# A hybrid diffusion-transformer step on one core: transposes by DMA on 16-bit halves, 33 groups of seven products, and new tables

## The chip, the cores and the metric

The kernel runs on one core of a Trainium2 chip. The metric is the device time of one execution in microseconds (us); before the change it is 1346.45 us, the median of three runs (1346.03 to 1346.79).

## The reference

One layer over two groups of 128 tokens of width 2048 (a prompt and a noisy sample), in float32:

```
(shift1, scale1, gate1, shift2, scale2, gate2) = SiLU(cond) @ w_ada + b_ada      # adaLN, per group
h  = RMSNorm(x) * (1 + scale1) + shift1
q_A, k_A, v_A, q_B, k_B, v_B, gate_A, gate_B = split(h @ w_in)                    # 8704 columns
o_A, o_B = two attentions (window / neighbourhood), with context keys
merged = (sigmoid(gate_A) * (o_A @ w_br_a) + sigmoid(gate_B) * (o_B @ w_br_b)) @ w_out
x  = x + gate1 * merged
h2 = RMSNorm(x) * (1 + scale2) + shift2
x  = x + gate2 * (relu(h2 @ w_up) ** 2 @ w_down)                                  # 2048 -> 8192 -> 2048
```

The outputs are both groups' x and the new keys and values.

## The kernel before, in words

**Steps.** All weights are streamed once, in 456 steps of one tile of 128 x 1024 numbers (512 KB: two rows of tiles of 128 x 512). For each step SP loads the tile `raw` (L208), ACT rounds it to the high half `wH` (`prep_hi`, through `copy`, L86), DVE subtracts to get the low half `wL` (`prep`, L234), and TensorE (PE) makes, for two k-tiles and both token groups, the three products high x high, high x low and low x high: 12 matmuls with 512 columns (`mm3`, L284 to 286; the first projections, `start_steps`, L384 to 386). Activations are stationary and are split in high and low as well; they must lie with features on the partitions, so each result that feeds a further product is transposed.

**Order.** The order on each engine is written out by hand. `run` goes through the steps; the strings `LOOK` and `RUN` (one digit per step) say how many steps ahead weights are split and loaded. A load has a key (its step less `LOAD` = 4) and goes out when the key is at most the step plus its `RUN` digit. Functions hung on a step by `at` are issued behind its matmuls. The steps: 0 to 71 first projections (nine units of 512 columns, in chunks of k), 72 to 135 the eight gate units, 136 to 167 the branches (`br_unit`, per n a unit of w_br_a and one of w_br_b), 168 to 199 w_out, 200 to 215 up units 0 and 1, and then in turn a pair of up units (16 steps, `up_pair`) and the w_down part of the pair before (four units of four steps, `down_unit`). All tiles of 4 KB per partition come from one pool of 48 buffers (`G`, `GEN`); a load waits on SP until the buffer that it gets is free.

**Transposes.** `tT` (L797 to L800) takes a unit's 2 x 128 x 512 result: eight 128 x 128 transposes on PE into two PSUM banks, then for each bank ACT copies the high half and DVE subtracts the low half. It serves the four merged units (`trans` in `br_unit`) and the 16 up units (`up_T`).

**Groups of seven.** In a pair of up units the eight groups of two k-tiles are either plain (two steps, eight products of three matmuls) or *fast*: seven products of three matmuls, after Strassen and Winograd, for which the weights are combined first (`prep_x`, `prep_y`, L1109 to L1133: four ACT copies, four DVE operations 1024 wide and three 512 wide). `FAST` lists, for each pair, the positions of the fast groups: 37 before. `w_upF` holds those weights in the needed order.

**Accumulating transfers.** For the steps in `LO_DMA` (and the fast groups in `XL_DMA`) ACT writes -wH and a transfer on GpSimd's queue adds the weights to it (`minus_plus`, L240, L241), in place of DVE's subtraction. For the units in `SUM_DMA` (4 p + n) the partial result of `down_unit` is copied by ACT and added by such a transfer (L1214), in place of DVE's two additions (L1210).

**adaLN.** Part of the modulation is a product on PE (`pair_load`: eight loads `araw`, `pair_mm`, L301; `ADA_AT` gives the step), and part are dot products on DVE (`dots`: rows `cB` of the condition, loaded five steps ahead of the first dot, SiLU, then a tile `aT` per dot of both groups, L1278); `DOTS1`, `DOTS` and `DOTS2` give their steps. `SS_AT` and `CONST_AT` place the second modulation's products and the constants.

**Gates away.** The gates in `AWAY` are stored to DRAM after their unit (L540) and fetched `GATE_BACK` steps before the end of the unit that uses them (L545).

Of the kernel before, what the change touches and what calls it, by code (L numbers as in the profile page):

```python
# [10 lines left out]
F32 = mybir.dt.float32  # L11
F32R = mybir.dt.float32r
BF16 = mybir.dt.bfloat16
AF = mybir.ActivationFunctionType
OP = mybir.AluOpType
AX = mybir.AxisListType

P = 128
# [10 lines left out]
PIECES = [[2 * i, 2 * i + 1] for i in range(8)]  # L29
# [14 lines left out]
LO_AHEAD = 2  # L44

LOOK = "523112344222344433223333332123333453344534332454455544344533333544324554444555556665556644444333333333332222122213444544555434333333342344333334333323445565533344456656533344434444445455564546555554444443322355444554433333333434334433333333333654654332334455554444555653323314333422222223443233333332223323365455454443222212233432443334434743443332222333423323333333333325434322223333433323333334555543365365433333332222554442122132334343222223332233345544"
RUN = "454562331000011222223333322222222222222233345555544455434445554445665555555664543433234334444445665543321222222212444444444444442222222232223344444455544544444444443344343334466644455555554543255444343355556866544443566553333323333345552332222222223445332333333333332211122222332233322211233323323332333223333333332343322211333343333322233333444433643333312222334443322333233322222222322333443434455544333120222222232111233456655566567556322325335553333333"
CONST_AT = [60, 65]
XL_DMA = [40]
ADA_AT = [None, 4, 13, 21, 21, 34, 30]  # L50
XS_AT = {1: 13, 2: 18, 3: 29}
POST = {('kvA', 0): [67, 69, 71], ('qA', 0): [70, 73, 75], ('qA', 1): [74, 76, 82], ('kB', 0): [78, 84, 89], ('qB', 0): [82, 84, 93], ('kB', 1): [85, 90, 93], ('qB', 1): [91, 94, 96]}
JOBS = [[78, 79, 81, 83, 94], [82, 83, 87, 90, 94], [88, 89, 91, 93, 98], [93, 93, 95, 98, 102], [96, 97, 100, 105, 112], [102, 103, 107, 112, 120], [105, 107, 111, 118, 120], [112, 114, 117, 120, 122]]
SS_AT = [48, 56, 66, 75, 139, 139]
T_AT = [4, 4]
PREP_IN = [6, 7]
DOTS = [32, 39, 41, 43, 47, 47, 48, 49, 51, 52, 53, 55, 60, 64, 67, 69, 72, 76, 76, 83, 89, 90, 92, 92, 94, 98, 101, 103, 103, 105, 108, 111, 111, 112, 115, 118, 120, 122, 123, 123, 124, 128, 129, 129, 131, 132, 133, 137, 137, 137, 138, 143, 144, 147, 147, 150, 153, 157, 158, 160, 165, 167, 168, 168, 170, 172, 175, 177, 177, 178, 179, 183]
DOTS2 = [232, 233, 235, 237, 240, 242, 262, 265, 269, 270, 272, 289, 297, 299, 302, 306, 307, 326, 327, 332, 334, 335, 358, 361, 364, 365, 368, 370, 393, 394, 397, 401]
STAT_AT = [-1, -1, 10, 12]
# [5 lines left out]
def tile_hybrid_step(ctx: ExitStack, tc: tile.TileContext, a):  # L65
# [3 lines left out]
    gp = ctx.enter_context(tc.tile_pool(name="gen", bufs=GEN))  # L69
# [15 lines left out]
    def copy(out, in_):  # L85
        act.activation(out, in_, AF.Copy)  # L86
# [14 lines left out]

    wm = G("wm", BF16)[:, 0:512]
    dve.memset(wm, 0.0)
# [82 lines left out]
    wsteps = []  # L186
    cal = {}

    def at(i, fn):
        cal.setdefault(i, []).append(fn)  # L190
# [357 lines left out]
    direct = {("gA", n) for n in DIRECT}  # L548
# [3 lines left out]
    def end_of(key):  # L552
        return max(st["i"] for st in wsteps if st["key"] == key)
# [224 lines left out]

    def sigmoids():
        for u in gates:  # L780
            if u not in direct:
                sigmoid(u)

    sig_at = end_of(("gA", DIRECT[0] - 1)) + 2
# [2 lines left out]


    mH, mL = [None] * 4, [None] * 4
    mt = {}  # L790

    def tT(src, hi, lo):

        for s in range(2):
            ps = bank("ps_T")
            for k in range(4):
                pe.transpose(ps[:, k * P:(k + 1) * P], src[:, s, k * P:(k + 1) * P], ident)  # L797
            psv = ps.rearrange("p (k t) -> p k t", k=4)
            copy(hi[:, :, s, :], psv)
            dve.tensor_tensor(lo[:, :, s, :], psv, hi[:, :, s, :].bitcast(F32), op=OP.subtract)  # L800

    def HL(name):
        return [G(name + x, F32R).rearrange("p (k s t) -> p k s t", k=4, s=2) for x in "HL"]

    def br_unit(n):
        def evac_a(acc):
            for s in range(2):
                dve.tensor_tensor(gates["gA", n][:, s, :], gates["gA", n][:, s, :], acc[s], op=OP.mult)

        def evac_b(acc):  # L810
            gb = gates.pop(("gB", n))
            ga = gates.pop(("gA", n))
            for s in range(2):
                dve.tensor_tensor(gb[:, s, :], gb[:, s, :], acc[s], op=OP.mult)
# [11 lines left out]
        at(end_of(("yb", n)) + 2, trans)  # L826

    br0 = len(wsteps)
    for n in range(4):
# [1 line left out]
    for u in AWAY:  # L831
        i = end_of(("y" + u[0][1].lower(), u[1]))
# [128 lines left out]
    split_unit(a["w_out"], 512 * 3, m_stat, evac_out3, ("out", 3), norm2_at(1, 0))  # L961


    aH, aL = {}, {}
    up_r = {}

    def h2_stat(j):
        return lambda kk, tb: (h2H[j][:, kk, tb, :], h2L[j][:, kk, tb, :])

# [15 lines left out]
        sync.dma_start(t, x1d[n])  # L985
        x1[n] = t.rearrange("p (s n) -> p s n", s=2)

    def up_T(n):
        aH[n], aL[n] = HL(f"a{n}")
        tT(up_r.pop(n), aH[n], aL[n])  # L990
# [12 lines left out]

# [54 lines left out]
    def up_pair(p):  # L1058
        n0, n1 = PIECES[p]
        w, box, key = a["w_up"], {"begun": set()}, ("up", n0)  # L1060
# [30 lines left out]
        for pos, is_fast in enumerate(kinds):  # L1091
            end = pos == 7
            if not is_fast:
                j = next(js)
# [10 lines left out]
            j = next(jf)  # L1105
# [36 lines left out]
            def mm_y(st, b=b, j=j, pos=pos, end=end):  # L1142
# [3 lines left out]
                lo, hi = slice(0, 512), slice(512, 1024)  # L1146
# [7 lines left out]
                if pos == 0:  # L1154
                    for name, stat, h, l in todo[0:3]:
                        mm(name, stat, h, l, end)
                    if p == 1:
                        up_T(PIECES[0][1])
# [110 lines left out]
    def dot(box, job, second, s, tag):  # L1269
# [59 lines left out]
    if first:  # L1329
        i = max(first[-1][0], H_AT - 1) + 1  # L1330
# [4 lines left out]
    i = 2 + max(i for i, (job, h, n) in placed if job[0] == "g1")  # L1335
# [4 lines left out]
    for c in range(FB_DVE // 2):  # L1340
        box = {}
        for j in range(2):
            i = SS_AT[2 * c + j]
# [7 lines left out]
    i = g2[-1][0] + 2  # L1351
# [3 lines left out]
    for n in range(4):  # L1355
        e = end_of(("down", last - 1, n))
# [3 lines left out]
    e = end_of(("out", 3))  # L1360
# [88 lines left out]
```

## Time and profile before

| what | us |
|---|---|
| median of three runs | 1346.45 |
| the profiled execution | 1346.98 |
| its span, first to last instruction | 1344.9 |
| PE busy | 1331.6 |
| DVE busy | 1194.9 |
| ACT busy | 738.8 |

The profile is of one execution. Busy times are sums over the span; a matmul's duration includes its way through the array, so matmuls overlap, and the distance between starts says what one costs. A line such as L86 or L797 is that of a helper through which many tiles go, so groups are told apart by the tile's name. In a row of waits the columns are: who waited, for whom, total us, times, longest us. In a row of groups: line, engine, operation, tiles, shapes, count, then busy us and mean ns, then idle time before it and what ended that. In a window's row: start and end, length, busy us and instructions of each engine, granted TensorE clock, DMA share, GB/s.

### The profile page before, as it was taken

What the parts mean: (1) busy time and instruction counts of PE and PEld (TensorE: products, weight loads), DVE (VectorE), ACT (ScalarE), POOL (GpSimd) and SP (SyncE); (2) the same over time, 40 slices, a digit from 0 to 9 for tenths busy, and PEclk for the clock granted to TensorE, in tenths of its full rate; (3) what the DMA queues carried; (4) which work ended last, traced back from release to release, by engine and by line L of the source; (5) the groups of instructions that cost most, each with busy time, mean ns of one, the idle gap of its engine ahead of it and who ended that gap; (6) DMA issues with size and microseconds to landing.
All of it is one profiled execution on the core that took longest, in us unless ns stands there. A gap on an engine that the chain in (4) does not pass through costs nothing.

```text
span 1344.9 us, 18331 instructions
## 1 busy us (share of the span) xinstructions
PE 1331.6 (99%) x6552; PEld 1081.6 (80%) x6552; DVE 1194.9 (89%) x1568; ACT 738.8 (55%) x966; POOL 66.7 (5%) x76
## 2 busy tenths in 40 slices
PE   8899999999999999999999999999999999999998
PEld 4577788888788878888888888888888888888887
DVE  4689999988898999998789999998999999899675
ACT  5524443566656544345666665565665656556540
POOL 0000001332000000000000000000000000000000
PEclk9899999999999999999999999999999999999999
DMA  9999998977688999798466666888798887769942
GB/s 370 410 409 408 404 366 352 375 215 271 193 282 299 377 397 344 284 332 290 175 232 230 240 219 245 271 264 279 231 317 239 265 285 216 267 191 302 373 151 93
DMA packets 109611, 385.44 MB, mean 287 GB/s; under 512 B 12368, under 2 KB 13584, under 8 KB 109520
## 3 DMA queue, kind: packets, MB, share of 16 engines
q1 hardware_dynamic: 104064, 365.05, 73.5%
q0 software_dynamic: 5312, 19.14, 7.5%
q8 instruction: 51, 0.84, 0.3%
q14 instruction: 40, 0.33, 0.1%
q10 hardware_dynamic: 144, 0.08, 0.0%
HBM read 369.25 MB, written 7.11 MB: 280 GB/s over the span
## 4 chain that ended last, share of the span: by engine, by line
PE 96%; DMA 3%; DVE 1%; issue 0%; ACT 0%; SPq 0%; DVEq 0%
PE acc L284 17%; PE acc L286 17%; PE acc L285 17%; PE Q L1068 6%; PE Q L1070 6%; PE Q L1069 6%; PE acc L384 4%; PE acc L386 4%; PE acc L385 4%; PE ps_ada L301 2%; DMA raw<-in_w_in 2%; PE ps_T L797 1%; PE ps_S L700 1%; DMA araw<-in_w_pair 1%; PE Z L1070 1%; PE Z L1069 1%
## 5 line engine op out<-in xcount | busy, mean ns | idle before, releaser
L234 DVE TENSOR_TENSOR wL<-raw,wH 128x1024 fp32r<-128x1024 f32 x361 | 430.7, 1225 | 79.6 <-ACT wH L86 72.6
L86 ACT ACTIVATE wH<-raw 128x1024 fp32r<-128x1024 f32 (+1 forms) x385 | 385.6, 1047 | 138.6 <-PE acc L285 33.0
L384 PE MATMUL acc<-wH,hH 128*128 128x512 f32 x276 | 109.9, 398 | 0.0
L386 PE MATMUL acc<-wH,hL 128*128 128x512 f32 x276 | 108.4, 393 | 0.7 <-DVE hL L90 0.7
L385 PE MATMUL acc<-wL,hH 128*128 128x512 f32 x276 | 108.5, 393 | 0.0
L284 PE MATMUL acc<-wH,hH 128*128 128x512 f32 x256 | 101.8, 398 | 0.0
L286 PE MATMUL acc<-wH,hL 128*128 128x512 f32 x256 | 99.8, 390 | 0.0
L285 PE MATMUL acc<-wL,hH 128*128 128x512 f32 x256 | 99.7, 389 | 0.0
L1278 DVE CUSTOM_DVE_ANT_0 aT<-aT,cB,cols 128x1024 f32<-128x1024 f32 x56 | 71.5, 1284 | 0.2
L1278 DVE CUSTOM_DVE_ANT_0 junk<-aT,cB,cols 128x1024 bf16<-128x1024 f32 x56 | 71.3, 1279 | 0.0
L86 ACT ACTIVATE tH<-t 128x1024 fp32r<-128x1024 f32 x37 | 39.3, 1062 | 56.9 <-DVE t L1123 42.0
L384 PEld LDWEIGHTS acc<-wH,hH 128*128 128x128 f32 x276 | 52.3, 190 | 14.2 <-issue 3.3
L386 PEld LDWEIGHTS acc<-wH,hL 128*128 128x128 f32 x276 | 52.4, 190 | 12.3 <-DVE hL L90 1.1
L385 PEld LDWEIGHTS acc<-wL,hH 128*128 128x128 f32 x276 | 52.4, 190 | 10.5
L86 ACT ACTIVATE uH<-raw 128x1024 fp32r<-128x1024 f32 x37 | 39.3, 1063 | 36.2 <-DVE raw L1128 35.2
L286 PEld LDWEIGHTS acc<-wH,hL 128*128 128x128 f32 x256 | 48.1, 188 | 10.3
L285 PEld LDWEIGHTS acc<-wL,hH 128*128 128x128 f32 x256 | 48.1, 188 | 9.6 <-issue 0.2
L284 PEld LDWEIGHTS acc<-wH,hH 128*128 128x128 f32 x256 | 48.1, 188 | 9.6 <-issue 0.2
L1123 DVE TENSOR_TENSOR t<-raw 128x1024 f32<-128x1024 f32 x37 | 45.1, 1220 | 5.8 <-PE Z L1069 1.9
L1176 ACT ACTIVATE up<-up 128x1024 f32<-128x1024 f32 x28 | 29.7, 1062 | 33.0 <-DVE up L1170 32.6
L86 ACT ACTIVATE dsum<-acc 128x512 f32<-128x512 f32 x38 | 22.0, 595 | 45.2 <-PE acc L286 42.1
L1133 DVE TENSOR_TENSOR uL<-raw,uH 128x1024 fp32r<-128x1024 f32 x37 | 45.1, 1219 | 0.1
(629 smaller groups left out, 3320.4 us busy)
## 6 DMA issues: line engine op xcount, KB each, us to landing
raw<-in_w_in SPq DMA_DIRECT2D x133, 512.0 KB, 6.7
raw<-in_w_down SPq DMA_DIRECT2D x128, 512.0 KB, 5.9
araw<-in_w_pair SPq DMA_DIRECT2D x80, 512.0 KB, 9.6
raw<-in_w_upF SPq DMA_DIRECT2D x74, 512.0 KB, 5.2
aT<-in_w_gT SPq DMA_DIRECT2D x64, 512.0 KB, 6.6
raw<-in_w_up SPq DMA_DIRECT2D x54, 512.0 KB, 5.1
aT<-in_w_adaT SPq DMA_DIRECT2D x48, 512.0 KB, 7.4
raw<-in_w_out SPq DMA_DIRECT2D x32, 512.0 KB, 9.5
```

What stands on the lines that cost most here:

```text
L86: act.activation(out, in_, AF.Copy)
L234: dve.tensor_tensor(st["lo"], st["raw"], st["hi"].bitcast(F32), op=OP.subtract)
L284: pe.matmul(acc[tb], sh, wh[:, k, :], start=f, stop=False)
L285: pe.matmul(acc[tb], sh, wl[:, k, :], start=False, stop=False)
L286: pe.matmul(acc[tb], sl, wh[:, k, :], start=False, stop=l)
L384: pe.matmul(acc[tb], sh, wh[:, k, :], start=kt == 0 and k == 0, stop=False)
L385: pe.matmul(acc[tb], sh, wl[:, k, :], start=False, stop=False)
L386: pe.matmul(acc[tb], sl, wh[:, k, :], start=False, stop=last and k == 1)
L1068: pe.matmul(acc, stat[0], hi, start=f, stop=False)
L1069: pe.matmul(acc, stat[0], lo, start=False, stop=False)
L1070: pe.matmul(acc, stat[1], hi, start=False, stop=l)
L1278: dve.tensor_tensor_reduce(out, box["raw"], cB[s, tag], 1.0, dst if second else baT[:, part, fb:fb + 1], OP.mult, OP.add, dst)
```

## The change

Every up unit, and the merge units 0 to 2 (all but those in `M_TE`), are transposed by a transfer. `part` writes the unit's float32 numbers as two planes of 16-bit halves (two ACT copies); `flip` transposes the planes' 128 x 128 blocks by one transposing transfer on SP; `join` puts the halves together again (an ACT copy of 2048 halves) and splits the result in high and low (ACT, DVE). The three are hung on steps by `M_AT`, `P_UP`, `T_UP`, `P_PAIR` and `T_PAIR`, with `FLIP` steps between `part` and `flip`.

```diff
-DOTS1 = [6, 8, 15, 20, 28, 30, 31, 38]
+DOTS1 = [11, 17, 20, 28, 28, 31, 34, 37]
-FAST = {1: (0, 1, 5, 6, 7), 2: (0, 3, 4, 6, 7), 3: (0, 2, 4, 5, 7), 4: (0, 2, 3, 5, 7), 5: (0, 1, 2, 4, 5, 7), 6: (0, 2, 4, 6, 7), 7: (0, 1, 2, 4, 5, 7)}
-SUM_DMA = [5, 6, 9, 10, 11, 12, 13, 15, 16, 19, 20, 21, 23, 25, 27]
-AWAY = [('gA', 1), ('gB', 0), ('gA', 2)]
-GATE_BACK = 3
+FAST = {1: (0, 3, 7), 2: (0, 2, 6, 7), 3: (0, 2, 4, 5, 7), 4: (0, 2, 4, 5, 7), 5: (0, 3, 4, 5, 7), 6: (0, 2, 4, 5, 7), 7: (0, 1, 2, 4, 5, 7)}
+SUM_DMA = [5, 6, 11, 13, 16, 19, 21, 23, 25, 27]
+AWAY = [('gA', 1), ('gB', 2), ('gB', 3), ('gA', 0), ('gB', 0), ('gA', 2)]
+GATE_BACK = 8
-LO_DMA = [70, 83, 86, 107, 131, 176, 184, 186, 196, 233, 242, 292, 314, 328, 357, 379, 402, 435]
+LO_DMA = [70, 83, 107, 131, 176, 184, 233, 292, 314, 328, 402, 404]
-CONST_AT = [60, 65]
-XL_DMA = [40]
-ADA_AT = [None, 4, 13, 21, 21, 34, 30]
+CONST_AT = [65, 67]
+XL_DMA = []
+ADA_AT = [None, 4, 13, 18, 21, 36, 29]
-SS_AT = [48, 56, 66, 75, 139, 139]
+SS_AT = [43, 51, 73, 75, 139, 139]
-T_PAIR = [[11, 11], [7, 15], [13, 13], [16, 16], [9, 9], [12, 12], [12, 12]]
+T_PAIR = [[8, 9], [6, 8], [8, 9], [7, 8], [10, 11], [8, 9], [12, 11]]
+P_PAIR = [[4, 2], [2, 4], [3, 4], [1, 3], [6, 6], [3, 3], [6, 5]]
+M_TE = (3,)
+M_AT = [1, 3, 9]
+FLIP = 1
+P_UP = [4, 1]
+T_UP = [6, 5]
...
+    def halves(key, name):
+        return gp.tile([P, 2048], U16, name=f"{name}{key[0]}{key[1]}", tag="g")
+    def part(key, src):
+        src = src.rearrange("p s (k f) -> p k s f", k=4).bitcast(U16).rearrange("p k s (f h) -> p h k s f", h=2)
+        planes[key] = halves(key, "pl")
+        dst = planes[key].rearrange("p (h k s f) -> p h k s f", h=2, k=4, s=2)
+        for h in range(2):
+            copy(dst[:, h], src[:, h])
+    def flip(key):
+        pl, planes[key] = planes[key], halves(key, "pT")
+        sync.dma_start_transpose(planes[key].rearrange("p (j t) -> p j t", t=P), pl)
+    def join(key, hi, lo):
+        full = G(f"fT{key[0]}{key[1]}")
+        copy(full.bitcast(U16).rearrange("p (c h) -> p h c", h=2), planes.pop(key).rearrange("p (h c) -> p h c", h=2))
+        split(hi.rearrange("p k s t -> p (k s t)"), lo.rearrange("p k s t -> p (k s t)"), full)
...
+        if n in M_TE:
+            at(end_of(("yb", n)) + 2, trans)
+        else:
+            e = end_of(("yb", n))
+            at(e + M_AT[0], lambda: part(("m", n), mt.pop(n)))
+            at(e + M_AT[1], lambda: flip(("m", n)))
+            at(e + M_AT[2], trans_end)
...
     def up_unit(n):
...
-        if n != PIECES[0][1]:
-            at(end_of(("up", n)) + 2, lambda: up_T(n))
+        at(end_of(("up", n)) + P_UP[n], lambda: up_planes(n))
+        at(end_of(("up", n)) + P_UP[n] + FLIP, lambda: up_flip(n))
+        at(end_of(("up", n)) + T_UP[n], lambda: up_T(n))
...
-            for n, i in zip(PIECES[p + 1], T_PAIR[p]):
-                at(len(wsteps) + i, lambda n=n: up_T(n))
+            for n, i, j in zip(PIECES[p + 1], P_PAIR[p], T_PAIR[p]):
+                at(len(wsteps) + i, lambda n=n: up_planes(n))
+                at(len(wsteps) + i + FLIP, lambda n=n: up_flip(n))
+                at(len(wsteps) + j, lambda n=n: up_T(n))
```

`up_planes`, `up_flip` and `up_T` call `part`, `flip` and `join` for an up unit. The strings `LOOK` and `RUN` are rewritten (most digits stay; the `RUN` digits of the first steps go from 4545623310000112 to 3011100000000102), and `POST`, `JOBS`, `DOTS`, `DOTS2` and `STAT_AT` are shifted by a few steps here and there. The sigmoid of the gates that went to DRAM is taken only where they come back.

More of the change, by code (lines that the diff above doesn't have):

```diff
@@ L13 @@
 BF16 = mybir.dt.bfloat16
+U16 = mybir.dt.uint16
 AF = mybir.ActivationFunctionType
@@ L50 @@
-ADA_AT = [None, 4, 13, 21, 21, 34, 30]
+LOOK = "443323444122344433223333332123333453344534333554455544344534333543324554444555556665556644444333333333332222122312344544555434333333342344333334333323445566643344456656533344434444445455564546555553444554322355444554433333333434334533333333333654544332334455543444555653215536544523333334543233333332223323365455455443222212233432443334434642333334444544534434333333333325434222223333434444444434555642255353443444442222432331122132223342112223332233345544"
@@ new lines @@
+RUN = "301110000000010212223333322222222221111122244455544355434445554334554445555664543433234334444445665543321222222212444444444444442222222232223344444455544544444444555455454445566644455555554543365434343355445756644443566664333312222234552332223333334545332333333333322211122222332233322212233323323332332112344444442343322211333343334323233334544422742222212223445554422333233322222211222333333435767545333110221112232111233456655566567556433435335553333334"
+CONST_AT = [65, 67]
+XL_DMA = []
@@ L55 @@
+JOBS = [[79, 80, 80, 87, 93], [81, 83, 88, 90, 93], [87, 87, 89, 90, 99], [93, 93, 96, 99, 102], [96, 97, 100, 105, 112], [102, 103, 107, 112, 123], [105, 107, 111, 118, 123], [112, 115, 118, 121, 123]]
+SS_AT = [43, 51, 73, 75, 139, 139]
 T_AT = [4, 4]
 PREP_IN = [6, 7]
[L57 removed]
@@ L61 @@
+DOTS2 = [230, 232, 234, 235, 236, 237, 240, 243, 255, 263, 265, 269, 270, 288, 301, 301, 307, 328, 328, 331, 333, 334, 358, 360, 361, 363, 366, 368, 391, 391, 395, 399]
+STAT_AT = [-1, 0, 10, 16]
+T_PAIR = [[8, 9], [6, 8], [8, 9], [7, 8], [10, 11], [8, 9], [12, 11]]
[5 more added lines that the diff above has]
+T_UP = [6, 5]
 COL = {"qA": 0, "kvA": 1024, "qB": 1536, "kB": 2560, "vB": 3584, "gA": 4608, "gB": 6656}
@@ L780, in sigmoids @@
         for u in gates:
-            if u not in direct:
+            if u not in direct and u not in AWAY:
                 sigmoid(u)
@@ L789, in tile_hybrid_step @@
     mH, mL = [None] * 4, [None] * 4
+    aH, aL = {}, {}
+    up_r = {}
     mt = {}
@@ L800, in tT, with up_planes, up_flip, up_T @@
             dve.tensor_tensor(lo[:, :, s, :], psv, hi[:, :, s, :].bitcast(F32), op=OP.subtract)
+    planes = {}
+    def halves(key, name):
[13 more added lines that the diff above has]
+        split(hi.rearrange("p k s t -> p (k s t)"), lo.rearrange("p k s t -> p (k s t)"), full)
+    def up_planes(n):
+        part(("a", n), up_r.pop(n))
+    def up_flip(n):
+        flip(("a", n))
+    def up_T(n):
+        aH[n], aL[n] = HL(f"a{n}")
+        join(("a", n), aH[n], aL[n])
     def HL(name):
@@ L825, in trans, with trans_end @@
             tT(mt.pop(n), mH[n], mL[n])
-        at(end_of(("yb", n)) + 2, trans)
+        def trans_end():
+            mH[n], mL[n] = HL(f"m{n}")
+            join(("m", n), mH[n], mL[n])
+        if n in M_TE:
[5 more added lines that the diff above has]
+            at(e + M_AT[2], trans_end)
     br0 = len(wsteps)
```

15 lines of the change are left out of this document (2 added, 13 removed).

## The prediction

> **What bounds the kernel now.** I read the page first (busy time, slices, chain), then the windows by stage, then the waits of PE, and last the groups by line for durations.
>
> ```profile
> span 1344.9 us, 18331 instructions
> PE 1331.6 (99%) x6552; PEld 1081.6 (80%) x6552; DVE 1194.9 (89%) x1568; ACT 738.8 (55%) x966; POOL 66.7 (5%) x76
> ...
> DMA  9999998977688999798466666888798887769942
> ...
> PE 96%; DMA 3%; DVE 1%; issue 0%; ACT 0%; SPq 0%; DVEq 0%
> ```
>
> PE is busy in all but 13.3 us of the span and makes up 96% of the chain that ended last. So what leaves PE's instruction stream shortens the run, as long as nothing else becomes late. The four stretches in which the edits fall, by windows:
>
> ```profile
> 110.00:260.00 150.00, 150.00 (x835) 119.11 (x834) 146.58 (x226) 63.61 (x76) 15.36 (x14) 1.00 0.97 378
> 420.00:592.00 172.00, 171.95 (x849) 142.00 (x848) 168.82 (x230) 81.34 (x96) 1.73 (x2) 1.00 0.95 351
> 592.00:860.00 268.00, 268.00 (x1220) 222.69 (x1219) 239.51 (x301) 164.45 (x209) 7.12 (x11) 1.00 0.69 239
> 860.00:1287.00 427.00, 427.00 (x1923) 354.24 (x1922) 392.08 (x452) 259.58 (x293) 17.84 (x21) 1.00 0.82 267
> ```
>
> Columns: length, PE, PEld, DVE, ACT, POOL busy, clock, DMA share, GB/s. In the first two stretches (first projections; branches and w_out) DVE is busy 98% of the time and DMA 95 to 97%: two more engines stand next to the limit. In the last two (MLP) DVE is at 89 and 92%, ACT at 61%, DMA at 69 and 82%. There PE is alone. PE's own waits:
>
> ```profile
> PE ps_ada L301 <- DMA araw<-in_w_pair: 4.2, 8, 0.7
> PE acc L454 <- ACT hH L86: 1.3, 2, 0.9
> ```
>
> They lie in the first 60 us, in the adaLN product of step 4.
>
> **The transposes that leave PE.**
>
> ```profile
> 545.66 0.87 PE ps_T L797 x8
> 1286.73 1.75 PE ps_T L797 x16
> ```
> ```profile
> L797 PE MATMUL ps_T<-ident,up x128: 270/272/273, 681.4 to 1288.2; 128*128 128x128 f32 x128
> L797 PE MATMUL ps_T<-ident,g_gA x32: 270/273/276, 500.2 to 568.9; 128*128 128x128 f32 x32
> L86 ACT ACTIVATE a3H<-ps_T x2: 622/628/635, 778.8 to 779.2; 128x512 fp32r<-128x512 f32 x2
> ```
>
> In the chain one unit, eight transposes, holds PE for 0.87 us (the 272 ns are pipelined, 0.11 us apart). All 128 of the MLP and 24 of the merge's 32 go: 19 units x 0.87 = **-16.5 us**. All of it stood on the chain.
>
> What comes instead, per unit: on ACT two copies of 1024 halves, a copy of 2048 halves and the high half of the split; on DVE one 1024-wide subtraction in place of two 512-wide ones from PSUM; on SP one transposing transfer of 512 KB.
>
> ```profile
> L86 ACT ACTIVATE wH<-raw 128x1024 fp32r<-128x1024 f32 (+1 forms) x385 | 385.6, 1047 | 138.6 <-PE acc L285 33.0 <-PE acc L385 22.0 <-PE acc L286 9.9
> L234 DVE TENSOR_TENSOR wL<-raw,wH 128x1024 fp32r<-128x1024 f32 x361 | 430.7, 1225 | 79.6 <-ACT wH L86 72.6 <-issue 2.6 <-PE ps_PT L746 2.6
> L1210 DVE TENSOR_TENSOR dsum<-dsum,acc 128x512 f32<-128x512 f32 x18 | 11.8, 683 | 3.4 <-PE acc L286 3.4
> ```
>
> ACT: 512 elements take 0.63 us and 1024 take 1.05, so 2048 about 1.9 (an estimate). 2 x 1.05 + 1.9 + 1.05 - 2 x 0.63 = +3.8 us per unit, 72 us in all. No row shows 16-bit elements two apart: at half these times it is 25 us, at twice 168 us. Even that leaves ACT at (739 + 168)/1330, 68%. I take the 72, cost nothing: it lies beside PE in stretches where ACT is 47 to 61% busy. DVE: 1.225 - 2 x 0.683 = -0.1 us per unit.
>
> The transfer. No row has one that transposes; the nearest are the gate's store and the slowest load of this size:
>
> ```profile
> gm_gA<-g_gA SPq DMA_DIRECT2D x2, 512.0 KB, 4.3
> bias<-in_rpb_qk SPq DMA_DIRECT2D x1, 512.0 KB, 10.2
> out_y_sample<-x1b SPq DMA_DIRECT2D x2, 128.0 KB, 1.9
> ```
>
> I take 4 to 10 us, as it is one transfer of the same bytes. The join comes 3 to 6 steps after the flip in the pairs (P_PAIR + 1 to T_PAIR), 6 in the merge, 1 and 3 in the first two up units, whose product is needed only twelve steps later. A step is 12 matmuls:
>
> ```profile
> 1298.53 0.39 PE L284 MATMUL acc<-wH,a14H 128*128 128x512 f32 x1
> 1299.21 0.39 PE L284 MATMUL acc<-wH,a14H 128*128 128x512 f32 x1
> ```
>
> Three matmuls in 0.68 us, so a step takes 2.7 us and three steps 8.2. A landing after 10 us is 2 us late, and LOOK has 3 to 5 further steps prepared (8 us at least). Two waits are new. The flip waits on SP for ACT's two copies, with the weight loads queued behind it. The join waits on ACT for the landing, with the wH copies behind it, then DVE's wL, then PE. While both stay under the 8 us of LOOK they cost nothing; without that cover each late microsecond is one of PE. A unit in flight also holds one or two more of the 48 buffers, and weight loads go out when buffers come free:
>
> ```profile
> SPq L208 <- PE acc L286: 257.6, 80, 9.3
> ```
>
> 80 loads waited for the matmuls that free their buffer. One or two buffers fewer shorten the run-ahead by as many steps, 2.7 to 5.5 us, for a few steps per unit; three more gates that lie in DRAM give three back during the merge. From nothing to those same microseconds once per unit: I take nothing, since the MLP's DMA is at 69 to 82% and can catch up.
>
> **Four groups of seven become plain.** FAST falls from 37 to 33: two groups in pair 1, one each in pairs 2 and 5. Seven products become eight, three matmuls each: 4 x 3 x 0.227 = **+2.7 us** of PE. DVE gains:
>
> ```profile
> L1123 DVE TENSOR_TENSOR t<-raw 128x1024 f32<-128x1024 f32 x37 | 45.1, 1220 | 5.8 <-PE Z L1069 1.9 <-PE Q L1069 1.7 <-DMA raw<-in_w_upF 1.2
> L1133 DVE TENSOR_TENSOR uL<-raw,uH 128x1024 fp32r<-128x1024 f32 x37 | 45.1, 1219 | 0.1
> L1126 DVE TENSOR_TENSOR raw<-t,raw 128x512 f32<-128x512 f32 x37 | 25.6, 692 | 1.3
> ```
>
> Four 1024-wide and three 512-wide operations, 4 x 1.22 + 3 x 0.69 = 6.9 us, become two wL, 2.45: -4.5 us each, -18.
>
> **Fewer accumulating transfers.** Of LO_DMA seven go and one (404) comes, XL_DMA's one and five of SUM_DMA go. Back on DVE: 7 x 1.22 + 10 x 0.683 = +15.4 us. By stretch: 592 to 860 us, DVE -13.5 + 3.7 against PE -4.4 + 2.0 (five units, three groups): 229 of 266, loose. 860 to 1287: -4.5 + 2.4 + 1.2 + 6.8 - 1 = 397, against PE 427 - 7.8 + 0.7 = 420: 95%, slack 23 us where it was 35. Tighter, still free: nothing counted. On DMA 12 accumulating transfers leave, 19 flips and six more gate transfers come; I call that even.
>
> **The branch stretch**, 420 to 592 us. Three merge units leave PE, so PE wants 169.4 us, and DVE keeps 168.4 with DMA at 0.95 and three more gate returns. Slack of 1 us in 170 is hardly met step for step. The 2.6 us that these units save may all come or not at all; I count half: **+1.3 us**.
>
> **The start.** The first dots move from step 6 to 11, so the two condition rows (cB, loaded five steps ahead of the first dot, key 1 to 6) and the first aT fall behind the eight adaLN blocks of step 4.
>
> ```profile
> 22.10 1.00 SPq L1256 DMA_DIRECT2D cB<-in_crow  x2
> 24.09 9.92 SPq L293 DMA_DIRECT2D araw<-in_w_pair  x8
> ```
> ```profile
> 36.20 0.64 PE L301 MATMUL ps_ada<-araw,cpad 128*32 128x256 f32 x8 [0.26 <-DMA araw<-in_w_pair]
> 37.47 0.64 PE L301 MATMUL ps_ada<-araw,cpad 128*32 128x256 f32 x8 [0.63 <-DMA araw<-in_w_pair]
> 43.85 1.08 PE L301 MATMUL ps_ada<-araw,cpad 128*32 128x256 f32 x8 [0.51 <-DMA araw<-in_w_pair]
> ```
>
> The blocks land 1.28 us apart and PE uses one in 0.64. Two transfers fewer ahead of them bring the last 2 x 1.28 = 2.6 us sooner: **-2.6 us**. Its ends: 0, if the bytes are merely owed later (the DMA line is at 9 in the first six slices, 200 us), and -6, if the clock also stays up (below). The silus and dots that move go to DVE at steps 8 to 37; DVE waits on raw weights around there, so I count them at nothing. The moved adaLN, constant and SS_AT loads are a reordering of the same bytes; in a full queue they can cost or gain about two transfers, 2.6 us, either way; I take nothing.
>
> **The sum.** Against the profiled execution: span 1344.9 - 16.5 + 2.7 + 1.3 - 2.6 = 1329.8; outside the span it had 1346.98 - 1344.9 = 2.1, so 1331.9; the median of the runs lies 0.5 under it: **1331.4 us**.
>
> **The rivals.** *The clock stays up at the start.*
>
> ```profile
> 43.00:44.00 1.00, 0.49 (x11) 0.15 (x8) 0.00 (x0) 0.00 (x0) 0.00 (x0) 0.50 1.05 414
> 49.00:50.00 1.00, 1.00 (x4) 0.72 (x3) 0.00 (x0) 0.60 (x1) 0.00 (x0) 0.59 1.03 410
> ```
>
> After 8 us of half-idle PE the granted clock is 0.50 for 6.5 us, which costs 3.2 us. With the waiting 2.6 us shorter it may not fall: 1328. For it: less waiting. Against: PE would still run half empty for some 5 us. [...]
>
> *DVE gives it back.* In the first two stretches DVE has 3 us of slack each, so neither the start's 2.6 nor the merge's other 1.3 us gets through, and the tighter MLP costs a further 2: 1337. For it: the 98%. Against: DVE's dead time before 110 us also shrinks when weights come sooner.
>
> *The flips are late* (slower). If a flip does not move as one transfer but as 16 blocks in a row, then with the least landing shown, 1.9 us, it takes up to 30 us. From 8.2 + 8.2 = 16.4 us on, each further microsecond stalls ACT, then PE, in 19 units; 13.8/19 = 0.7 us past that eats the gain. At 20 us it is 19 x 3.6 = 68 us, so 1400; at 30 us about 1590. For it: no row of a transposing transfer at all. Against: its bytes are those of a load. [...]
>
> **Chances.** Forecast (1327 to 1336) 0.57; clock stays up (1322 to 1327) 0.12; DVE gives back (1336 to 1343) 0.16; late flips 0.12; between 1343.8 and 1349, small lateness, 0.03. The range 1323 to 1343 leaves out the last two and a little at the bottom. A measurement of this kernel tells 0.2%, 2.7 us, from no change: faster 0.85, same 0.03, slower 0.12.
>
> **What would show it.** Right: PE busy near 1316 us, no ps_T of up tiles, flips landing under 10 us, PE's waits still a few us and all before 60 us. Step by step: ACT near 800 us, its waits on the transposed tile short; DVE near 1190; the clock slice of 40 to 50 us tells the start. Wrong: PE waiting on wL or wH shortly after a join, SP waiting on ACT's plane copies with weights landing late, or a flip held for over 16 us.

## The result, and the profile after

The changed kernel takes 1333.28 us (median of four runs, 1332.59 to 1333.46) against 1346.24 us for the kernel before, run beside it (four runs, 1344.17 to 1346.79): a ratio of 0.9906, 95% interval 0.9888 to 0.9923. The forecast was 1331.4. The profiled execution took 1333.11 us, its span is 1331.3; all differences below are between spans, or between starts in the traces.

The lines of the page that answer to those of before (busy time, the DMA slices, the chain, packets and the largest queue):

```profile
span 1331.3 us, 18039 instructions
PE 1316.0 (99%) x6411; PEld 1067.0 (80%) x6412; DVE 1190.2 (89%) x1546; ACT 800.8 (60%) x979; POOL 54.6 (4%) x64
...
DMA  9999998986589999996578876988798696878962
...
DMA packets 148267, 392.24 MB, mean 295 GB/s; under 512 B 51793, under 2 KB 53009, under 8 KB 148177
...
q1 hardware_dynamic: 144448, 378.16, 78.8%
...
PE 92%; DMA 4%; DVE 2%; ACT 1%; issue 1%; SPq 0%; DVEq 0%; ACTq 0%
```

PE is still busy for all but 15.3 us, but its share of the chain fell from 96 to 92%, and DMA, DVE and ACT now stand in it. The four stretches again, by windows (columns as ahead of the prediction):

```profile
110.00:260.00 150.00, 149.75 (x829) 118.56 (x828) 147.00 (x217) 62.59 (x73) 16.70 (x17) 1.00 0.97 377
420.00:592.00 172.00, 172.00 (x834) 141.88 (x833) 169.77 (x230) 95.48 (x102) 2.60 (x3) 1.00 1.02 373
592.00:860.00 268.00, 267.89 (x1199) 221.85 (x1197) 237.47 (x293) 184.04 (x214) 4.29 (x7) 1.00 0.73 246
860.00:1275.00 415.00, 411.01 (x1803) 338.97 (x1804) 381.54 (x433) 284.92 (x292) 10.40 (x12) 1.00 0.84 269
```

Only the last one has lost more than 0.3 us of PE time: 4.0 us in 415. Here are PE's two largest waits, and then, by windows, the two moments at which it waited or ran slowly (around 40 us and around 1199 us):

```profile
PE Q L1117 <- ACT dsum L93: 4.0, 2, 3.6
PE ps_ada L308 <- DMA araw<-in_w_pair: 2.5, 5, 0.6
```
```profile
40.00:50.00 10.00, 9.36 (x55) 7.11 (x48) 5.70 (x10) 8.17 (x12) 0.00 (x0) 1.00 1.03 409
1190.00:1200.00 10.00, 6.40 (x28) 5.04 (x27) 9.90 (x11) 5.99 (x9) 0.00 (x0) 0.97 0.46 161
1200.00:1210.00 10.00, 10.00 (x39) 8.09 (x39) 9.93 (x11) 6.49 (x9) 0.87 (x1) 0.86 0.90 268
```

At the start the clock now stays at 1.00 where the kernel before had this:

```profile
40.00:50.00 10.00, 8.18 (x44) 4.67 (x45) 2.36 (x2) 3.08 (x4) 0.00 (x0) 0.66 1.03 408
```

At 1199 us a new wait of 3.6 us stands, with the clock down behind it. The path to it is in the timelines of PE, ACT and DVE (start, us, what, and in brackets the idle time before):

```profile
1195.58 0.39 PE L1119 MATMUL Q<-YB,h20L 128*128 128x512 f32 x1
1199.57 0.80 PE L1117 MATMUL Q<-tH,sH 128*128 128x512 f32 x1 [3.60 <-ACT dsum L93]
1200.16 0.63 PE L1118 MATMUL Q<-tL,sH 128*128 128x512 f32 x1
```
```profile
1176.07 2.53 ACT L93 ACTIVATE fTa<-pTa 128x2048 uint16<-128x2048 uint16 x1
1178.64 1.06 ACT L93 ACTIVATE a12H<-fTa 128x1024 fp32r<-128x1024 f32 x1
1179.76 2.51 ACT L93 ACTIVATE fTa<-pTa 128x2048 uint16<-128x2048 uint16 x1
1182.30 1.06 ACT L93 ACTIVATE a13H<-fTa 128x1024 fp32r<-128x1024 f32 x1
...
1197.97 1.06 ACT L93 ACTIVATE uH<-raw 128x1024 fp32r<-128x1024 f32 x1 [1.00 <-DVE raw L1177]
1198.94 1.06 ACT L93 ACTIVATE dsum<-acc 128x512 f32<-128x512 f32 x2
```
```profile
1179.73 1.23 DVE L97 TENSOR_TENSOR a12L<-fTa,a12H 128x1024 fp32r<-128x1024 f32 x1 [1.81 <-ACT a12H L93]
1183.40 1.22 DVE L97 TENSOR_TENSOR a13L<-fTa,a13H 128x1024 fp32r<-128x1024 f32 x1 [2.44 <-ACT a13H L93]
```

The path is read backwards. PE wants to open two new banks (accumulators in PSUM). They are freed by the two copies `dsum<-acc` of the last w_down unit before. These stand on ACT behind the copies tH and uH of weights that are prepared five steps ahead. Those wait for DVE, which works without a pause from 1183 to 1200 us. Just before, DVE had stood idle for 1.81 + 2.44 = 4.25 us, because two joins came one behind the other and held ACT for 7.3 us (1176.07 to 1183.36). By this reading the joins are paid for some 16 us later, through three engines; the experiments below test it.

The flips on SP: first the duration of the 16 MLP flips' instruction (least, median and greatest, in ns), then the time to landing of all 19, then what the flips waited for on SP:

```profile
  L828 SPq DMA_TRANSPOSE pTa<-pla x16: 1778/3184/8667, 676.3 to 1258.8; - x16
...
DMA to landing us min/median/max: 4.2/5.7/10.7
```
```profile
SPq L828 <- ACT wH L93: 36.1, 11, 4.9
...
SPq L828 <- ACT pla L93: 18.6, 4, 6.9
SPq L828 <- PE acc L292: 17.2, 5, 6.6
```

The joins and the plane copies on ACT:

```profile
L93 ACT ACTIVATE fTa<-pTa 128x2048 uint16<-128x2048 uint16 x16 | 40.5, 2533 | 2.0 <-PE acc L292 1.4 <-DMA pTa<-pla 0.5
L93 ACT ACTIVATE pla<-up 128x1024 uint16<-128x1024 uint16 x32 | 31.7, 1043 | 1.7 <-PE acc L292 1.7
```

The transposing transfer lands after 5.7 us in the middle, and ACT waited 0.5 us in all for `pTa`. SP stood still for 72 us in all ahead of flips (the three rows), with weight loads queued behind, yet PE's only wait of more than 0.4 us behind 60 us is the one at 1199 us, and that is not for a load.

The gains by place, from the first matmul that uses a tile (such rows as this one of before and the one of after below it): branches −6.08 us (468.54 to 462.46), w_out −8.77, pair 1 −9.65, then −10.29, −11.71, −12.78, −13.70 at the w_down parts 1 to 4, −15.42 at part 5, −11.95 at part 6, and −13.6 at the end (the spans).

```profile
  L284 PE MATMUL acc<-wH,a10H x32: 389/389/476, 1166.1 to 1205.4; 128*128 128x512 f32 x32
```
```profile
  L291 PE MATMUL acc<-wH,a10H x32: 389/389/389, 1150.6 to 1188.3; 128*128 128x512 f32 x32
```

Where the 13.6 us come from: transposes −16.5, four plain groups +2.7, the start −6.1 (forecast −2.6), and new waits +6.3, which is what is left over (at 1199 us 3.6 of waiting and 1.7 of half clock; the other 1.0 was not followed). The theory to be tested: the steps of the sum are real; the start gained more, as the clock stayed up; and the joins' lateness gave back nearly as much in one place.

Part of the start's gain may belong to the execution and not to the kernel. In 33 executions of the kernel before, made beside the experiments, the mean granted clock is 0.999 or more in nine, with a mean span of 1342.4 us, and 0.997 or less in 14, with 1344.3. The profiled one (0.997, 1344.9) is of the second sort, so about 2 us of the 13.6 may hang on whether the old kernel's clock falls; the record doesn't say at what moment it fell in the others.

### The profile page after: what moved, and what is told of

It reads as the page before. It is cut to its first block, busy times and chain, and to the rows that moved or that the text cites. A ratio compares the mean times of both kernels' runs of the same rounds, so it can differ in the third digit from the quotient of the medians.

```text
span 1331.3 us, 18039 instructions
## 1 busy us (share of the span) xinstructions
PE 1316.0 (99%) x6411; PEld 1067.0 (80%) x6412; DVE 1190.2 (89%) x1546; ACT 800.8 (60%) x979; POOL 54.6 (4%) x64
## 3 DMA queue, kind: packets, MB, share of 16 engines
q1 hardware_dynamic: 144448, 378.16, 78.8%
## 4 chain that ended last, share of the span: by engine, by line
PE 92%; DMA 4%; DVE 2%; ACT 1%; issue 1%; SPq 0%; DVEq 0%; ACTq 0%
PE acc L291 16%; PE acc L292 16%; PE acc L293 16%; PE Q L1117 6%; PE Q L1119 6%; PE Q L1118 6%; PE acc L391 4%; PE acc L392 4%; PE acc L393 4%; DMA araw<-in_w_pair 3%; PE ps_ada L308 2%; PE ps_S L707 1%; PE Z L1119 1%; PE Z L1117 1%; PE Z L1118 1%; DMA aT<-in_w_adaT 1%
## 5 line engine op out<-in xcount | busy, mean ns | idle before, releaser
L241 DVE TENSOR_TENSOR wL<-raw,wH 128x1024 fp32r<-128x1024 f32 x375 | 446.6, 1225 | 72.0 <-ACT wH L93 67.9
L93 ACT ACTIVATE wH<-raw 128x1024 fp32r<-128x1024 f32 (+1 forms) x393 | 392.8, 1044 | 128.3 <-PE acc L392 23.3
L93 ACT ACTIVATE tH<-t 128x1024 fp32r<-128x1024 f32 x33 | 35.0, 1061 | 58.0 <-DVE t L1172 55.4
L391 PEld LDWEIGHTS acc<-wH,hH 128*128 128x128 f32 x276 | 51.8, 188 | 13.6 <-issue 2.5
L93 ACT ACTIVATE uH<-raw 128x1024 fp32r<-128x1024 f32 x33 | 35.1, 1063 | 31.6 <-DVE raw L1177 28.6
L308 PE MATMUL ps_ada<-araw,cpad 128*32 128x256 f32 x640 | 39.1, 382 | 2.7 <-DMA araw<-in_w_pair 2.5
L93 ACT ACTIVATE fTa<-pTa 128x2048 uint16<-128x2048 uint16 x16 | 40.5, 2533 | 2.0 <-PE acc L292 1.4
L1172 DVE TENSOR_TENSOR t<-raw 128x1024 f32<-128x1024 f32 x33 | 40.2, 1219 | 1.0 <-PE acc L292 1.0
```

The costliest lines, as they stand in the source:

```text
L241: dve.tensor_tensor(st["lo"], st["raw"], st["hi"].bitcast(F32), op=OP.subtract)
L391: pe.matmul(acc[tb], sh, wh[:, k, :], start=kt == 0 and k == 0, stop=False)
```

## The experiments

All kernels are the changed one with the edit named, except where it says "the kernel before". Ratios are to the kernel before, with the 95% interval. The kernel before ran beside each of the three groups of experiments, with medians of 1344.91, 1345.53 and 1346.10 us; the changed kernel was timed only beside the result, so differences to it hold to about 1 us. Of the eleven edits of the changed kernel, eight have intervals that overlap its own (0.9888 to 0.9923): all but the pairs' units, the joins drawn apart and the 37 groups. What is said of the eight rests on the ranges of their runs, each of which lies wholly above or below 1332.59 to 1333.46, and on starts in the traces.

**The start: the old steps of the first dots.**

```diff
-DOTS1 = [11, 17, 20, 28, 28, 31, 34, 37]
+DOTS1 = [6, 8, 15, 20, 28, 30, 31, 38]
```

> The changed kernel with the steps of the first dots as before (first dot at step 6, the rest of the new tables kept). Theory: the two condition rows and the first aT go out ahead of the adaLN blocks again, PE waits some 2.6 us longer in step 4 and the clock falls as before: the start loses about 6 us, 1339 in all. Rival: the start was won by the other tables (RUN, LOOK, adaLN steps): under 1 us, 1333 to 1334.

1335.5 us, 0.9929 (0.9913 to 0.9946); span 1333.8, +2.5 on the changed kernel; at the branches it is 3.1 late. Its window around 40 us:

```profile
40.00:50.00 10.00, 8.60 (x55) 4.76 (x56) 3.00 (x7) 4.67 (x7) 0.00 (x0) 0.83 1.03 408
```

The clock fell again, for about half as long as before, and its waits on `araw` were 3.8 us against 2.5: 1.3 of waiting and 1.7 of half clock. So the later dots bring about half of the start's 6.1 us, between the theory (about 6) and the rival (under 1). The other half goes with the rest of the new tables, or with the clock of the execution of before; no run parts the two.

**The same edit on the kernel before.** The old kernel with the new `DOTS1` and nothing else.

> The kernel before with nothing but the first dots moved (first at step 11). Theory (the two condition rows and one aT ahead of the adaLN blocks cost the start 2.6 us of waiting, and the clock's fall another 3.2): the first projections end 3 to 6 us sooner, 1340.5 to 1343.5 in all. Rival (only together with the other tables): under 1 us, or slower.

1345.35 us (ten runs), 0.9999 (0.9990 to 1.0008): no difference. Yet the gain is there at first. The matmuls of step 10, at 62 us, come 6.4 us sooner than before, with the clock at 1.00 throughout. It is given back bit by bit: 0.7 us by 116 us, 2.8 between there and 165, and 1.9 at 181 us, where PE now waits for DVE's low half; 1.06 us are left at the branches. These are PE's waits from 62 to 260 us, where the kernel before has none:

```profile
PE ps_ada L301 <- DMA araw<-in_w_pair: 1.8, 3, 0.6
PE acc L385 <- DVE wL L234: 1.6, 1, 1.6
PE ps_sel L319 <- ACT S L86: 0.6, 1, 0.6
```

The first two losses begin with loads and not with DVE. At the later adaLN products, at 100 us and from 145 to 147, PE waits for the loads `araw`, and at 150 us for a copy on ACT, which had itself waited 6.30 us for a load of weights. In starts that takes back 3.5 us (DMA's share is 1.03 from 90 to 110 us and 1.02 from 140 to 150, by windows). The same late weights leave DVE idle for 4.07 us up to 149 us; from 157 to 190 us it has no pause of more than 0.2 us in which to make that good, and the last 1.9 us are lost at 181 us. So the gain goes the way of one end of the start's range in the prediction (0, "if the bytes are merely owed later"), and the rival "DVE gives it back" holds for the last third of it. In the changed kernel, with `ADA_AT`, `RUN` and the other tables new, the waits for `araw` in that stretch are 0.3 us, and the gain is kept (−6.57 at 62 us, −6.08 at the branches).

**The merge units on PE again.**

```diff
-M_TE = (3,)
+M_TE = (0, 1, 2, 3)
```

> The changed kernel with all four merge units transposed on PE again. Theory (the branch stretch lets the whole saving through): 3 x 0.87 = 2.6 us come back, 1335.9, seen as 2.6 us between the start of the branches and the start of w_out. Rival (DVE at 98% sets the pace there, as I counted for half of it): 0 to 1.3 us, 1333.3 to 1334.6.

1336.03 us, 0.9934 (0.9920 to 0.9949); span 1334.4. Between the branches' start and w_out it loses 2.69 us, 0.90 per unit, and at the end 3.1. So in the changed kernel the three units' whole 2.6 us get through, though DVE and DMA read 99 and 102% there between 420 and 592 us (98 and 95% in the kernel before, which has the units on PE).

**The pairs' units on PE again** (14 units; the merge and the first two up units stay transfers).

```diff
-            for n, i, j in zip(PIECES[p + 1], P_PAIR[p], T_PAIR[p]):
-                at(len(wsteps) + i, lambda n=n: up_planes(n))
-                at(len(wsteps) + i + FLIP, lambda n=n: up_flip(n))
-                at(len(wsteps) + j, lambda n=n: up_T(n))
+            for n, j in zip(PIECES[p + 1], T_PAIR[p]):
+                at(len(wsteps) + j, lambda n=n: up_T_pe(n))
```

> The changed kernel with the 14 units of the pairs transposed on PE again, at the steps of the joins; up units 0 and 1 and the merge keep the transfers. Theory: 14 x 0.87 = 12.2 us come back on PE and the wait at pair 7 (5.3 us with the half clock) goes with the joins: +7 to +12, 1340 to 1345. Rival (the wait at pair 7 belongs to the tables, not to joins and transfers): the full 12.2, 1345.5.

1340.73 us, 0.9963 (0.9948 to 0.9977); span 1338.8, +7.45. At a2H, a4H, a6H, a8H, a10H it stands at +1.78, +3.47, +5.74, +7.35 and +9.10 on the changed kernel: ten units, 0.91 each, near the 0.87 from the chain. At a12H it is +5.76: the wait at 1199 us is not there. ACT is busy for 742.2 us against 800.8, so a unit by transfer costs ACT 58.6 / 14 = 4.2 us more.

```profile
PE acc L292 <- DVE wL L241: 0.5, 1, 0.5
```

This is PE's longest wait behind the first 60 us. So the 3.6 us belong to the transposes by transfer.

**The transfers left out.** The flip is not issued and the join reads the planes as they are, so this kernel leaves the transposition out, and with it the flip's target buffer.

```diff
-        pl, planes[key] = planes[key], halves(key, "pT")
-        sync.dma_start_transpose(planes[key].rearrange("p (j t) -> p j t", t=P), pl)
+        pass
```

> The changed kernel without the transposing transfers: the join reads the planes as they are, so the transposition and its target buffer are left out and the numbers are not the reference's. Theory (PE's new wait of 3.6 us in pair 7 comes from two joins in a row on ACT, the transfers themselves are hidden): the wait stays, 1332 to 1333.5. Rival (two transfers that hold SP for 9.35 us make the loads and then the splits late): the wait and the half clock behind it go, 1327 to 1329.

1330.88 us, 0.9896 (0.9881 to 0.9911); span 1328.4, −2.9. Before pair 7 it is 0.8 ahead; the rest comes at the wait of 1199 us, which shrinks, and the mean granted clock is 0.999 in place of 0.998, which leaves no room for the 1.7 us of half clock:

```profile
PE Q L1116 <- ACT dsum L93: 2.3, 1, 2.3
```
```profile
q1 hardware_dynamic: 104928, 368.20, 74.3%
```

So the transfers with their buffers cost 2.9 us in all, 0.8 over the whole run and 2.1 at that one place. The wait is 2.3 us without them and, by the run before this one, gone without the planes and joins as well: the larger part of it comes from the work on ACT and not from the transfers, which lengthen it by 1.3 us. Theory and rival each hold in part.

**The two joins drawn apart.** Entry 5 of the list, that of units 12 and 13, is joined at steps 7 and 12 in place of 8 and 9.

```diff
-T_PAIR = [[8, 9], [6, 8], [8, 9], [7, 8], [10, 11], [8, 9], [12, 11]]
+T_PAIR = [[8, 9], [6, 8], [8, 9], [7, 8], [10, 11], [7, 12], [12, 11]]
```

> The changed kernel with the two joins ahead of pair 7 apart: steps 7 and 12 of that down part in place of 8 and 9. Theory (ACT's 7.2 us of joins in a row starve DVE): DVE's idle 4.2 us there shrink, PE's wait of 3.6 us and the 1.6 us of half clock go, 1328 to 1330. Rival (the SP queue): unchanged, 1333.

1337.62 us, 0.9943 (0.9928 to 0.9958); span 1333.9, +2.6: a miss. The profiled execution is the fastest of the four; by medians it is +4.3.

```profile
PE ps_gr L1340 <- DVE gc_g L1327: 4.2, 1, 4.2
PE Q L1117 <- ACT dsum L93: 2.4, 1, 2.4
```

The old wait shrank by 1.2, and a new one of 4.2 us came, which ended at 1181.6 us: the join at step 7 put `a12L` on DVE ahead of the last dot product that a product on PE needs. The first join must not be sooner; the place is tight on both sides.

**One digit of LOOK.** Weights at step 406 are prepared four steps ahead in place of five, so that the bank-freeing copies are no longer behind them.

```diff
-LOOK[400:412] = "422553534434"
+LOOK[400:412] = "422553434434"
```

> The changed kernel with one digit of LOOK smaller: at step 406 weights are prepared up to step 410 in place of 411. Theory (the order on ACT: the copies that free the two PSUM banks of the last unit of that down part are issued behind tH and uH of pair 7's second group, and those wait for DVE, which the two joins made late): ACT frees the banks 4 to 5 us sooner, PE's wait of 3.6 us and the 1.6 us at half clock go, 1328 to 1329.5. Rival (PE would wait for the second group's weights a step later anyway, since DVE is late): within 1 us of 1333.

1330.88 us, 0.9887 (0.9871 to 0.9904); span 1329.7.

```profile
PE Q L1118 <- DVE XL L1180: 1.5, 2, 1.3
...
PE Q L1117 <- DVE dsum L1257: 0.7, 1, 0.7
```
```profile
1194.47 1.28 ACT L93 ACTIVATE dsum<-acc 128x512 f32<-128x512 f32 x2 [0.62 <-PE acc L293]
...
1196.32 1.06 ACT L93 ACTIVATE tH<-t 128x1024 fp32r<-128x1024 f32 x1
```

The two copies that free the banks now stand ahead of tH and 4.5 us sooner. The 3.6 us are gone and the clock stays up (1.000 in the mean, 0.998 in the changed kernel): a12H starts 2.51 us sooner than in the changed kernel. But 1.3 us of waiting for DVE come in the same pair, and 0.7 behind it, so 1.7 are left at the end. Both theories hold by half: the order on ACT made the wait of 3.6 us, behind which the clock went down, and DVE is truly late by 1 to 2 us.

**Three more digits** (279 from 5 to 3, 310 from 5 to 4, 311 from 5 to 3), for the small waits of other pairs.

> The digit of the run before, and three more at the same place of pairs 3 and 4 (steps 279, 310 and 311), where PE waits 0.3 and 0.6 us for a bank. Theory: 0.5 to 1 us under the run with one digit, 1327.5 to 1329. Rival: those short waits come back as waits for weights, no difference.

1331.22 us, 0.9888 (0.9874 to 0.9903); span 1329.4. Against one digit the span is 0.3 less and the median 0.3 more: not to be told apart, as the rival said.

**37 groups again**, the lists of before in pairs 1, 2 and 5, all other tables as in the changed kernel.

```diff
-FAST = {1: (0, 3, 7), 2: (0, 2, 6, 7), 3: (0, 2, 4, 5, 7), 4: (0, 2, 4, 5, 7), 5: (0, 3, 4, 5, 7), 6: (0, 2, 4, 5, 7), 7: (0, 1, 2, 4, 5, 7)}
+FAST = {1: (0, 1, 5, 6, 7), 2: (0, 3, 4, 6, 7), 3: (0, 2, 4, 5, 7), 4: (0, 2, 4, 5, 7), 5: (0, 1, 2, 4, 5, 7), 6: (0, 2, 4, 5, 7), 7: (0, 1, 2, 4, 5, 7)}
```

> The changed kernel with 37 groups of seven again (two more in pair 1, one more each in pairs 2 and 5). Theory (DVE has room there): PE saves 4 x 0.68 = 2.7 us, 2.0 of it by the end of pair 2, 1330.6 in all. Rival (seven DVE operations in place of two, and ten buffers a group in place of four, make PE wait for weights in those pairs): nothing gained or slower, 1333.3 to 1337.

1347.81 us (ten runs, 1343.14 to 1350.79), 1.0009 (0.9997 to 1.0022); span 1349.0, +17.7, where PE's own work is 2.7 us less. The profiled execution is the slowest of the ten; by medians it is +14.5. All of the gain is gone, and the time is far above the rival's range too.

```profile
PE Q L1117 <- ACT dsum L93: 4.4, 3, 3.6
PE Q L1117 <- DVE dsum L1257: 3.0, 1, 3.0
PE acc L291 <- ACT up L93: 3.0, 1, 3.0
...
PE acc L291 <- DVE up L1217: 2.3, 3, 1.5
```

PE is idle for 28.0 us against 15.3, and the clock falls at more places than one (0.83 from 730 to 740 us and again from 870 to 880; 0.995 in the mean, against 0.998). A fast group costs DVE 4.5 us more than a plain one and saves PE 0.7; beside the joins that is not covered here. Between 690 and 920 us PE waits for DVE for 5.4 us and for ACT for 4.5, and the half clock at those two places takes 1.7 each: the loss is +6.9 us by a1H and +13.5 by a4H. The edit also moves the places of the fast groups, and the tables were not made anew for 37, so this says what 37 cost with these tables, not with the best ones.

**The accumulating transfers of before.**

```diff
-SUM_DMA = [5, 6, 11, 13, 16, 19, 21, 23, 25, 27]
+SUM_DMA = [5, 6, 9, 10, 11, 12, 13, 15, 16, 19, 20, 21, 23, 25, 27]
-LO_DMA = [70, 83, 107, 131, 176, 184, 233, 292, 314, 328, 402, 404]
+LO_DMA = [70, 83, 86, 107, 131, 176, 184, 186, 196, 233, 242, 292, 314, 328, 357, 379, 402, 435]
-XL_DMA = []
+XL_DMA = [40]
```

> The changed kernel with the accumulating transfers of before (LO_DMA, SUM_DMA and XL_DMA as they were): DVE is relieved of 15.4 us, SP, GpSimd and the DMA engines get 12 transfers more. Theory (giving them up was free): within 0.7 us of 1333.3. Rival (DVE's tightness after 860 us is what the short waits and the wait at pair 7 come from): 1 to 4 us faster, 1329 to 1332.

1336.65 us, 0.9931 (0.9915 to 0.9948); span 1335.6, +4.3. At 45 to 62 us it loses 1.6 us, of which 1.1 are left before any edited step acts: in this execution the clock fell there for some 3.4 us (0.77, 0.50 and 0.88 in the windows of 2 us from 40 to 46), with the same instructions as in the changed kernel, so that is not the edit's. The other 3.2 come mostly in pair 7:

```profile
PE Q L1117 <- ACT dsum L93: 3.8, 2, 3.5
...
PE ps_gr L1340 <- DVE gc_g L1327: 1.6, 1, 1.6
```

From 860 to 1275 us DVE has 369.45 us of work in place of 381.54 and ACT 290.12 in place of 284.92, and DMA's share is 0.88 in place of 0.84; yet the waits became more, not fewer, and the clock stayed down for 6.8 us behind the wait of 3.5 us, not 3.4 (0.90, 0.50, 0.50, 0.50 and 0.89 in the windows of 2 us from 1200 to 1210). Neither theory had it slower. The new wait of 1.6 us for the last dot product on DVE and 1.7 us more of half clock make up about what pair 7 loses. LOOK and the other tables had been made for the shorter lists; why the dot comes later there was not tried by itself.

**Two versions that use what was found.** Both have the four LOOK digits; the first also puts the joins of units 12 and 13 at steps 8 and 11, the second takes one XL from DVE by a transfer.

```diff
-T_PAIR[5] = [8, 9]
+T_PAIR[5] = [8, 11]
```
```diff
-XL_DMA = []
+XL_DMA = [56]
```

> The four LOOK digits of the earlier run, and the second join ahead of pair 7 at step 11 in place of 9, so that the first stays where it was. Theory (DVE's idle 2.4 us between the two joins is what is left of the wait): the waits of 1.4, 0.4 and 0.7 us in pair 7 and behind it shrink, 1329 to 1330. Rival (the second join then holds up pair 7's first groups on ACT): 1331 to 1334.

> The four LOOK digits, joins as in the change, and the low half of pair 7's first X made by an accumulating transfer, which takes 1.22 us from DVE and gives ACT 1.06. Theory (DVE is what is late in pair 7): the wait of 1.4 us for XL and the 0.4 behind it go, 1329.5 to 1330.5. Rival (ACT's extra copy or the landing takes its place): 1331 or more.

1330.91 us, 0.9889 (0.9875 to 0.9904), span 1328.5; and 1330.62 us, 0.9889 (0.9874 to 0.9904), span 1328.6. The largest of PE's waits behind the start in the second, and what is left of the one for XL:

```profile
PE acc L292 <- DVE wL L241: 1.1, 2, 0.6
...
PE Q L1118 <- DMA XL<-in_w_upF: 0.3, 1, 0.3
PE Q L1118 <- DVE uL L1182: 0.2, 1, 0.2
PE Q L1118 <- DVE XL L1180: 0.2, 1, 0.2
```

In the second the wait for DVE's XL is nearly gone, and 0.3 us of waiting for the transfer stand in its place. Both times lie between what the theories and the rivals gave (1329 to 1330 or 1331 to 1334; 1329.5 to 1330.5 or 1331 and more), so neither is settled.

Both beat the kernel before, and by medians the changed one (by 2.4 and 2.7 us) as well; the intervals of the ratios to the kernel before overlap, so against the changed kernel this rests on the spans (−2.8 and −2.7) and medians. Against the run with one digit of LOOK (1330.88 us) they are not told apart: the one digit brings what all of them bring.

## Why the prediction was right, point by point

- **PE bounds the kernel.** Right: PE busy 1316.0, as forecast, and what left PE's stream shortened the run. But "PE's waits all before 60 us" failed, with the 3.6 us at 1199 us.
- **Transposes −16.5.** Right: 0.91 per unit in the pairs, 0.90 in the merge, by putting them back; forecast 0.87.
- **Flips and joins hidden.** The transfer was nearly right: 4.2 to 10.7 us to landing (forecast 4 to 10), 0.5 us of waiting for it on ACT, and 0.8 us of run time in all outside the one bad place. ACT was right in its sum (800.8 us, forecast near 800), though the copy of 2048 halves took 2.53 us, not the estimated 1.9, and a unit 4.2 us and not 3.8. (The bounds of 25 and 168 us there also scaled the float32 copy of the high half, whose time is in the rows; with the 16-bit copies alone they are 34 and 148.) What failed is "While both stay under the 8 us of LOOK they cost nothing": the joins of units 12 and 13 came one behind the other and held ACT for 7.3 us, which is under 8; DVE lost 4.25 us, and PE 3.6 and 1.7 of half clock. An average of 60% on ACT said nothing of 7.3 us held in one piece, and the cover was not LOOK alone but also the order on ACT: a deeper LOOK put weight copies ahead of the copies that free PE's banks, and one digit less took the 3.6 us away.
- **Four plain groups +2.7.** The term is not disputed, but the step missed what the groups were for: with 37 and these tables the loss is 14.5 us by medians (17.7 in the profiled execution). The 18 us that they give DVE were in my working and were priced at nothing.
- **Accumulating transfers, "tighter, still free: nothing counted".** Right in that giving them up cost nothing; wrong in that with these tables it was a gain, about 3 us (3.2 by the traces, 3.4 by medians).
- **The branch stretch +1.3.** Wrong: all of the 2.6 came (2.69 measured). DVE, busy for 169.8 of 172 us, did not hold PE back there.
- **The start −2.6.** Mis-sized: −6.1. Of my two rivals there, "the clock stays up" happened: 1.7 us less waiting for `araw`, and no half clock in the profiled execution. How far the fall itself is luck is open: the kernel before has executions at a clock of 0.999 and more, and one of the changed kernel's first steps, in the run with the accumulating transfers of before, has the fall.
- **The sum.** 1331.4 forecast, 1333.28 measured: the start and the branches gave 4.8 us more than I had, the new waits took 6.3, and the errors nearly cancel: the span came 1.5 us above the 1329.8 of the sum. The mechanism on PE was right; that the time was so near is partly luck.
- **The rivals.** "DVE gives it back" did not happen in the changed kernel. Where the dots alone were moved, the gain was given back, but 3.5 us of it to loads that came late, and only the last 1.9 to DVE. "Late flips" did not: the landing of all 16 blocks is 4.2 to 10.7 us.

What stays open: which of the new tables keeps the start's gain (the loads of the adaLN tiles are the likeliest place) and how much of it is the clock's luck, the last 1.0 us of the new waits, and why the accumulating transfers of before are slower.

## What to carry to other kernels

Work that moves off the bounding engine to one with room by its average must still be placed so that two pieces of it do not stand together: look for the longest stretch that they hold an engine, and follow what is queued behind it, through two engines if need be. Work that frees the bounding engine's buffers should stand ahead of work that is merely prepared early (shown here at one place; three more such edits changed nothing). And an edit that looks like a price (plain groups) may be a condition of the gain: undo it alone, with the rest in place, before calling it a loss. Nor is a gain at the start kept of itself: where the DMA queue is full, what is loaded later must be followed to the place where it is used.

## What the runs showed of the hardware

- **Where the clock fell, it was at 0.50 for about 3.4 or 6.8 us.** In windows of 1 and 2 us the lowest clock is 0.50, so the time at it is twice the missing share: kernel before, 10 x 0.34 x 2 = 6.8 us; old dots, 10 x 0.17 x 2 = 3.4; changed kernel at 1199 us, (0.3 + 1.4) x 2 = 3.4; the accumulating transfers of before, 3.4 at 40 us and 6.8 at 1202. In the changed kernel it followed one gap of 3.6 us, with 37 groups one of 3.0 (the fall at 736 us); with the transfers left out, where the longest gap behind the start is 2.3 us, the mean granted clock is 0.999. The run with the joins apart, with gaps of 4.2 and 2.4 us, reads 0.998 in the mean, as the changed kernel does. At the start it fell with no gap above 0.7 us, and with the same first steps it fell in one execution (0.83 from 40 to 50 us, with the accumulating transfers of before) and not in another (1.00, the changed kernel). So the length of a gap does not by itself part the falls from the rest; what does, no run here shows.
- **A transposing transfer of 512 KB lands much like a plain one (5.7 us in the middle, plain loads of the MLP's weights 5.0 to 5.6), but is dearer on the queues.** It holds SP for 3.2 us in the middle, up to 8.7 (the 16 of the MLP). Left out, the 19 flips take 39,520 packets with them (144,448 less 104,928), 2,080 each, of some 250 bytes (9.96 MB in all). The queue's time falls by 0.788 x 1331.3 − 0.743 x 1328.4 = 62 us of all 16 engines, 3.3 per flip; what is left on that queue takes 1.4 us per 512 KB (0.743 x 1328.4 us for 368.20 MB).
- **ScalarE's copies of 16-bit elements two apart**: 1024 read so take 1.04 us, like 1024 in float32 (1.05). 2048 written so take 2.53 us, a fifth more than twice that.
